# Channel-major copies of the input rows for the first RMSNorm of a hybrid encoder layer, in place of transposes on TensorE

## The chip, the cores and the metric

The kernel runs on one core of a Trainium2 chip. The metric is the device time of one execution in microseconds (us). Three runs of the kernel before took 3526.61, 3523.47 and 3514.22 us; the median is 3523.47 us. The engines are called as the profile calls them: PE is TensorE (PEld its weight loads), DVE VectorE, ACT ScalarE, POOL GpSimd, and SP the engine whose queue issues most of the DMAs.

## The reference

The reference is one layer over two streams, a prompt of 16 learned meta tokens and 2048 new rows, and a sample stream of 64 rows that goes on from given states. Rows have 1024 channels.

```python
def _rmsnorm(x, w):
    y = xf * lax.rsqrt(jnp.mean(jnp.square(xf), -1, keepdims=True) + EPS)
    return (y * w.astype(F32)).astype(x.dtype)
...
m, ns = _mixer(_rmsnorm(x, p['norm1_w'][l]), l, *st, segs, p)
x = x + m
x = x + _swiglu(_rmsnorm(x, p['norm2_w'][l]), p['w_gate'][l], p['w_up'][l], p['w_down'][l])
```

`_mixer` begins with one product of the normed rows with `w_in` (1024 x 5384). Its columns go to three groups of heads (Mamba-2 SSD, RWKV-7, HGRN2), whose outputs are normed, joined, and mapped back by `w_out`. A SwiGLU feed-forward network with 2816 hidden channels and a last RMSNorm follow. The change touches only the first RMSNorm and the way its result reaches the product with `w_in`.

## The kernel before

The 2128 rows are cut into 17 tiles: tile 0 holds the 64 sample rows and the 16 meta rows, tiles 1 to 16 hold 128 prompt rows each. Tiles are gathered into six chunks of 336, 384, 384, 384, 384 and 256 rows, and chunks into three blocks of two.

All large products run in split single precision: each operand is kept as a rounded part `hi` and a remainder `lo`, and PE adds `hi*hi + hi*lo + lo*hi`. A weight unit (128 x 512) is loaded from HBM as `raw` (line 219), rounded by ACT (line 220), and its remainder is taken by POOL for three units of four and by DVE for the fourth (line 222). The split copy is stored to HBM (line 224) and read back when the unit is used again (line 216). There are three `raw` buffers and five for split units.

A chunk goes to the projection as `hT`, a pair of tiles `hhi` and `hlo` with channels on the partitions, 8 groups of 128 channels by up to 384 rows. `Chunk.load` makes it from row tiles with rows on the partitions. For each tile, ACT squares the rows and sums them (line 237); DVE and POOL turn the sum into `(mean + eps)^-0.5` (lines 228 and 230); DVE multiplies the rows by that factor and by the norm's weights, which a DMA has laid down on all partitions (line 246); PE transposes eight blocks of 128 x 128, four to a PSUM bank (line 252); ACT rounds each bank into `hhi` (line 254) and DVE writes the remainder to `hlo` (line 255). A chunk of three tiles has 24 transposes. The pool of PSUM banks `g` has four banks, for the projection's sums and the transposes together.

The row tiles come by DMA on SP's queue (line 144) into three buffers `x`. `Chunk.fetch` asks for the three tiles of a chunk.

`projection` writes the order of the work down: for block 0, the first four column tiles (the "head") of chunk 0, then the load of chunk 1, the head of chunk 1, then the other column tiles with each weight unit used for both chunks. At the end of a block the gate columns `z` are computed, and the load of the next block's first chunk is woven into them. The load of the second chunk of a block comes after the `v` columns of the first. While the projection runs, two streams of mixer work are stepped in between by a table of estimated costs. Below that, a planner that keeps an estimated timeline orders the instructions of each engine and of the DMA queues; priority goes by the order in which the program is written. So an edit in one place can reorder rows on every engine.

SP's queue is in order: where a DMA has to wait until its target buffer is free or its source is written, the DMAs behind it wait as well.

## Time and profile before

| | |
|---|---|
| median of three runs | 3523.47 us |
| time of the profiled execution | 3511.97 us |
| its span in the trace | 3510.2 us |
| mean granted clock of PE | 0.982 |
| busy share: PE, PEld, DVE, ACT, POOL | 96%, 84%, 63%, 35%, 22% |
| DMA over the span | 860.42 MB, 245 GB/s |

The profiled execution is one of the program's faster ones: its own time is 11.5 us under the median, and lies 1.8 us over its span. In the prediction the sum is made against 3511.97 us and then moved up by 11.5 us. A line number in the profile is a line of the kernel; line 111 is the helper through which every product goes, so its groups have to be told apart by the names of their tiles. A name on the left of the arrow is what an instruction writes, the names on the right are what it reads, with the moving operand of a product first.

### The profile page before, as it was taken

How to read it: one execution, taken by the hardware profiler on the slowest of the kernel's cores; microseconds unless marked ns; L12 is line 12 of the kernel's file. 1: busy time of each engine (PE TensorE's matmuls, PEld its weight loads, DVE VectorE, ACT ScalarE, POOL GpSimd, SP SyncE). 2: the span in 40 equal slices, each digit the busy share in tenths (PEclk: the TensorE clock that was granted, in tenths of full speed). 3: DMA queues.
4: the chain of work that ended last, by engine and by line, in shares of the span. 5: the costliest groups of instructions: out<-in, count | busy, mean ns of one | idle time of the engine just before them, and what ended most of it. 6: DMA issues, size and time to landing. Idle time of an engine off the chain costs nothing.

```text
span 3510.2 us, 61013 instructions
## 1 busy us (share of the span) xinstructions
PE 3366.0 (96%) x22588; PEld 2942.8 (84%) x22588; DVE 2212.6 (63%) x4961; ACT 1226.9 (35%) x2635; POOL 778.5 (22%) x1122
## 2 busy tenths in 40 slices
PE   7999999999999998899898999999999999999998
PEld 7999789999799996787787888888988887888786
DVE  3358555567665677687877767667643676665453
ACT  4445233344343443343452212223210352233342
POOL 3324201102112112344442211111100123431101
PEclk9999999999999998899999999999999999999999
DMA  9776875565775667889889898686788567875856
GB/s 321 233 227 209 298 237 160 172 180 163 247 223 173 193 194 245 288 305 315 293 303 346 297 328 275 227 285 203 224 259 267 199 209 263 304 273 165 295 191 215
DMA packets 427123, 860.42 MB, mean 245 GB/s; under 512 B 112432, under 2 KB 212280, under 8 KB 424776
## 3 DMA queue, kind: packets, MB, share of 16 engines
q1 hardware_dynamic: 394376, 749.01, 64.9%
q0 software_dynamic: 32448, 107.50, 8.4%
q8 instruction: 178, 2.92, 0.3%
q14 instruction: 121, 0.99, 0.1%
HBM read 603.81 MB, written 252.54 MB: 244 GB/s over the span
## 4 chain that ended last, share of the span: by engine, by line
PE 69%; DMA 11%; DVE 10%; issue 4%; ACT 2%; POOL 2%; SPq 2%; POOLq 0%; DVEq 0%; ACTq 0%
PE g L111 47%; PE d L111 11%; PE c L111 5%; PE h L111 4%; DMA w<-w 3%; DMA raw<-in_w_up 1%; DMA hin<-hg 1%; POOL w L222 1%; DMA hg<-stage 1%; DVE tp L640 1%; DVE Xp L641 1%; DMA raw<-in_w_gate 1%; PE po L111 1%; DVE acc L1278 1%; DVE gcv L418 1%
## 5 line engine op out<-in xcount | busy, mean ns | idle before, releaser
L111 PE MATMUL g<-hhi,w 128*128 128x384 f32 (+3 forms) x3312 | 831.7, 330 | 10.1 <-POOL w L222 3.7
L111 PEld LDWEIGHTS g<-hhi,w 128*128 128x128 f32 (+1 forms) x3312 | 580.0, 188 | 23.9 <-POOL w L222 4.5
L111 PE MATMUL g<-h2hi,w 128*128 128x384 f32 (+1 forms) x2112 | 548.6, 335 | 21.9 <-DMA w<-w 7.9
L111 PE MATMUL g<-hlo,w 128*128 128x384 f32 (+3 forms) x1680 | 550.5, 328 | 0.0
L111 PEld LDWEIGHTS g<-h2hi,w 128*128 128x128 f32 x2112 | 376.4, 190 | 35.2 <-ACT w L220 8.6
L111 PE MATMUL g<-h2lo,w 128*128 128x384 f32 (+1 forms) x1056 | 349.6, 331 | 0.0
L111 PEld LDWEIGHTS g<-hlo,w 128*128 128x128 f32 (+1 forms) x1680 | 314.1, 187 | 6.2
L222 POOL TENSOR_TENSOR w<-raw,w 128x512 fp32r<-128x512 f32 x180 | 244.0, 1358 | 338.3 <-ACT w L220 276.3
L111 PE MATMUL g<-w,mhi 128*128 128x512 f32 x792 | 259.3, 404 | 8.3 <-DMA w<-w 3.5
L220 ACT ACTIVATE w<-raw 128x512 fp32r<-128x512 f32 x240 | 150.1, 628 | 194.2 <-PE g L111 50.0
L111 PEld LDWEIGHTS g<-h2lo,w 128*128 128x128 f32 x1056 | 200.3, 190 | 2.8
L111 PE MATMUL g<-w,hhi 128*128 128x512 f32 (+1 forms) x544 | 178.1, 407 | 7.4 <-DMA w<-w 4.2
L111 PEld LDWEIGHTS g<-w,mhi 128*128 128x128 f32 x792 | 145.0, 189 | 43.6 <-DVE acc L1278 4.5
L640 DVE TENSOR_TENSOR tp<-Xp,b4k 128x60 f32<-128x60 f32 (+24 forms) x527 | 125.1, 237 | 52.0 <-DMA b4k<-psc 38.9
L1278 DVE TENSOR_TENSOR acc<-g,acc 128x512 f32<-128x512 f32 (+1 forms) x198 | 132.1, 682 | 39.2 <-PE g L111 38.9
L111 PE MATMUL g<-w,mlo 128*128 128x512 f32 x396 | 155.7, 394 | 0.0
L111 PE MATMUL g<-w,op 128*128 128x512 f32 x600 | 142.8, 395 | 0.0
L111 PEld LDWEIGHTS g<-w,op 128*128 128x128 f32 x600 | 112.3, 187 | 27.3
L641 DVE TENSOR_TENSOR Xp<-Xp,tp 128x60 f32<-128x60 f32 (+24 forms) x527 | 122.9, 233 | 13.3
L230 POOL TENSOR_TENSOR rs<-ss,half 128x1 f32<-128x1 f32 (+2 forms) x51 | 34.6, 681 | 424.6 <-DVE ss L228 261.0
L111 PEld LDWEIGHTS g<-w,hhi 128*128 128x128 f32 (+1 forms) x544 | 99.5, 189 | 32.4 <-DMA w<-w 6.5
L356 DVE SCALAR_TENSOR_TENSOR stage<-graw,cvec,stage 128x384 f32<-128x384 f32 (+2 forms) x98 | 53.5, 549 | 113.5 <-ACT graw L351 34.4
(449 smaller groups left out, 6619.2 us busy)
## 6 DMA issues: line engine op xcount, KB each, us to landing
w<-w SPq DMA_DIRECT2D x893, 512.0 KB, 4.4
hin<-hg SPq DMA_DIRECT2D x16, 1280.0 KB, 7.7
rin<-rw SPq DMA_DIRECT2D x16, 896.0 KB, 6.2
raw<-in_w_gate SPq DMA_DIRECT2D x56, 256.0 KB, 4.4
raw<-in_w_up SPq DMA_DIRECT2D x56, 256.0 KB, 4.3
hg<-stage SPq DMA_DIRECT2D x64, 192.0 KB, 2.5
raw<-in_w_out SPq DMA_DIRECT2D x48, 256.0 KB, 4.4
sin<-ss SPq DMA_DIRECT2D x16, 768.0 KB, 4.9
```

Source lines behind the costliest of these rows:

```text
L111: return T.matmul(out, lhsT, rhs, start=start, stop=stop, skip_group_check=more)
L220: S.activation(hi, raw, AF.Copy)
L222: (G if units[0] % 4 < GLO else V).tensor_tensor(lo, raw, wt[:, 0], SUB)
L230: G.tensor_tensor(rs[:n], ss[:n], half[:n, 0:w], ALU.pow)
L356: V.scalar_tensor_tensor(st[:, a0:a1], raw[:, s0:s0 + a1 - a0], mu, st[:, a0:a1], MUL, ADD)
L418: V.scalar_tensor_tensor(cvt[:, :M], raw[:, j:j + M], tap(j), cvt[:, :M], MUL, ADD)
L640: V.tensor_tensor(tv, _bc(Xp[:, 0:m, q], 2, w), _bc(Up[:, q, q + 1:32], 1, m), MUL)
L641: V.tensor_tensor(Xp[:, 0:m, q + 1:32], Xp[:, 0:m, q + 1:32], tv, ADD)
L1278: V.tensor_tensor(self.acc[:n, i, cs], ps[:n], self.acc[:n, i, cs], ADD)
```

## The change

Each chunk's input rows are laid down in HBM a second time by the host, transposed: `xt0` to `xt5`, with channels on the partitions. `Chunk.fetch` now starts two kinds of load. The row tiles go, as before, through SP's queue, but one after the other into a single buffer `xq` (for chunk 0 into three buffers `b4k`); ACT squares each in place and leaves only the sums of squares `xss`. The transposed rows go by two DMAs into one buffer `xT` for a whole chunk.

`Chunk.load` turns all sums of a chunk into factors at once (one POOL power). For each tile, DVE multiplies the identity by the factors (a diagonal 128 x 128 matrix); PE multiplies a matrix of ones by it, which puts the factor of every row on all partitions; ACT copies that out of PSUM as `rb`. For each of the eight channel groups DVE multiplies `xT` by the norm's weight of the channel and by `rb`; for each pair of groups ACT rounds into `hhi` and DVE writes the remainder to `hlo`. The diagonal and `rb` take two of the three `stage` buffers, which also carry projection results to their stores. The buffer that held the norm's weights on all partitions is gone; they are columns of the constants `cvec` now. The matrix of ones is made ahead of the first load.

```diff
-    def fetch(tiles):
...
+    def squares_of(tiles, buf):
+        ss = mk(gp, [P, 4], tag="xss", bufs=2)
...
+        for j, t in enumerate(tiles):
+            xt = buf()
             for src, r0, n in x_rows(t):
                 nc.sync.dma_start(xt[r0:r0 + n], src)
-            xs.append(xt)
-        return xs
+            xt = xt[:LEN[t]]
+            S.activation(xt, xt, AF.Square, accum_out=ss[:LEN[t], j:j + 1])
+        return ss
+    def turned_rows(ci):
+        xT = mk(gp, [P, KD, CW], tag="xT", bufs=1)
+        n = sum(LEN[t] for t in CHUNKS[ci])
+        for k in range(0, KD, 4):
+            nc.sync.dma_start(xT[:, k:k + 4, :n], A[f"xt{ci}"][:, k:k + 4])
+        return xT
...
-    x0 = fetch(CHUNKS[sbs[0][0]][:1])
-    nw1 = norm_rows(gp, "norm1")
+    c0 = sbs[0][0]
+    ss0 = squares_of(CHUNKS[c0], lambda: mk(mx, [P, 1024], tag="b4k", bufs=3))
+    xT0 = turned_rows(c0)
...
         def fetch(self):
-            self.x = fetch(self.tiles)
+            self.ss = squares_of(self.tiles, lambda: mk(gp, [P, D], tag="xq", bufs=1))
+            self.xT = turned_rows(self.ci)
         def load(self):
             hi, lo = self.hT = [mk(gp, [P, KD, CW], F32R, tag=tag, bufs=2) for tag in ("hhi", "hlo")]
-            hs = [(xt[:, :512], xt[:, 512:]) for xt in self.x]
+            N, xT, ss = self.N, self.xT, self.ss
+            nt = self.nt
+            V.tensor_scalar(ss[:, :nt], ss[:, :nt], 1.0 / D, EPS, MUL, ADD)
+            rs = mk(gp, [P, 4], tag="xrs", bufs=2)
+            G.tensor_tensor(rs[:, :nt], ss[:, :nt], half[:, 0:nt], ALU.pow)
+            dg, rb = by(self.stage(), P), self.stage()
             for j, n in enumerate(self.lens):
-                o = self.offs[j]
-                rms_scaled(gp, self.x[j], n, nw1, hs[j], hi[:n, :, o:o + P])
-                yield 0.0
-                for k4 in range(2):
-                    transposed(hs[j][k4], k4, n, hi, lo, o, gbank)
-                    yield 0.5
+                V.tensor_scalar(dg[:n, j, :n], ident[:n, :n], rs[:n, j:j + 1], None, MUL)
+            yield 1.0
+            ps = gbank()
+            for j, n in enumerate(self.lens):
+                mm(ps[:, self.offs[j]:self.offs[j] + n], ones[:n], dg[:n, j, :n], True, True)
+            S.activation(rb[:, :N], ps[:, :N], AF.Copy)
+            yield 1.0
+            for k in range(0, KD, 2):
+                for i in (k, k + 1):
+                    V.scalar_tensor_tensor(xT[:, i, :N], xT[:, i, :N], c("norm1")[:, i:i + 1], rb[:, :N], MUL, MUL)
+                S.activation(hi[:, k:k + 2, :N], xT[:, k:k + 2, :N], AF.Copy)
+                V.tensor_tensor(lo[:, k:k + 2, :N], xT[:, k:k + 2, :N], hi[:, k:k + 2, :N].bitcast(F32), SUB)
+                yield 1.0
```

How the order of the instructions moves is shown at three places. In the changed kernel line 146 is the row load, 156 the load of the transposed rows, 231 the load of a raw weight unit, 236 the store of a split one, 329 the mean, 334 the diagonal, 343 the product with `rb`, 345 the remainder, and 379 the last step of a column tile of the RWKV group.

The first place is SP's queue while the head of chunk 0 is computed. Before, from the second raw unit on:

```order
L219 DMA raw_330<-in_w_rw 128x512
L219 DMA raw_363<-in_w_rw 128x512
L144 DMA x_517<-in_x_prompt 128x1024
L144 DMA x_519<-in_x_prompt 128x1024
L144 DMA x_521<-in_x_prompt 128x1024
L224 DMA w_315<-w_310 128x1024
L219 DMA raw_382<-in_w_rw 128x512
L224 DMA w_367<-w_362 128x1024
L224 DMA w_334<-w_329 128x1024
L219 DMA raw_415<-in_w_rw 128x512
L219 DMA raw_434<-in_w_rw 128x512
```

The same place in the change, in two pieces: from the second raw unit on, and from the eighth raw unit on.

```order
L231 DMA raw_303<-in_w_rw 128x512
L231 DMA raw_336<-in_w_rw 128x512
L146 DMA xq_491<-in_x_prompt 128x1024
L236 DMA w_288<-w_283 128x1024
L231 DMA raw_355<-in_w_rw 128x512
L156 DMA xT_500<-in_xt 128x1536
...
L231 DMA raw_407<-in_w_rw 128x512
L146 DMA xq_494<-in_x_prompt 128x1024
...
L231 DMA raw_459<-in_w_rw 128x512
L146 DMA xq_497<-in_x_prompt 128x1024
```

Before, the three row tiles of chunk 1 left together ahead of the fourth raw unit; now the second follows the sixth raw unit and the third the eighth, with both halves of the transposed rows in between.

The second place is DVE at the load of chunk 1. Before (`x_517`, `x_519` and `x_521` are its three row tiles, `hlo_524` its remainder):

```order
L246 SCALAR_TENSOR_TENSOR x_517<-x_517,rs_57_528,nw_85 128x512 x2
L228 TENSOR_SCALAR ss_546<-ss_546 128x1
L246 SCALAR_TENSOR_TENSOR x_519<-x_519,rs_61_549,nw_85 128x512 x2
L228 TENSOR_SCALAR ss_567<-ss_567 128x1
L246 SCALAR_TENSOR_TENSOR x_521<-x_521,rs_65_570,nw_85 128x512 x2
...
L255 TENSOR_TENSOR hlo_524<-g_532,hhi_523 128x4x128
L255 TENSOR_TENSOR hlo_524<-g_539,hhi_523 128x4x128
```

The same load in the change:

```order
L329 TENSOR_SCALAR xss_490<-xss_490 128x3
L334 TENSOR_SCALAR stage_508<-ident,xrs_506 128x128 x3
L379 SCALAR_TENSOR_TENSOR stage_478<-graw_477,cvec,stage_478 128x64
L379 SCALAR_TENSOR_TENSOR stage_478<-graw_477,cvec,stage_478 128x272
L343 SCALAR_TENSOR_TENSOR xT_500<-xT_500,cvec,stage_509 128x384 x8
L345 TENSOR_TENSOR hlo_504<-xT_500,hhi_503 128x768 x4
```

All eight products with `rb` now stand ahead of the first remainder, and nothing of the chunk starts before the sums of all three tiles are there.

The third place is PE at the load of chunk 5 in the change; `g_10606` receives the factors, `hhi_10597` and `hlo_10598` are the chunk's parts, `g_10675` and `g_10676` its first sums:

```order
L111 MATMUL h_10524<-us_10434,onesr 128x256 x2
L111 MATMUL h_10532<-Sss,sin_10167 128x256 x2
L111 MATMUL g_10606<-stage_10602,onesr 128x128 x2
L111 MATMUL h_10631<-us_10338,us_10247 128x256 x2
L111 MATMUL g_10675<-w_10677,hhi_10597 128x512 x2
L111 MATMUL g_10676<-w_10677,hhi_10597 128x512 x2
L111 MATMUL h_10701<-us_10626,onesr 128x512
L111 MATMUL h_10701<-us_10627,onesr 128x512
L111 MATMUL g_10675<-w_10677,hlo_10598 128x512
```

Where 16 transposes of the chunk stood, 15 of them close together ahead of its first products, there are now two products with ones. The row tiles of chunks 2 to 5 move the other way: their loads and squares stand on SP and ACT within the first part of block 0, since they need no other buffer than `xq`.

More of the change, by code (lines that the diff above doesn't have):

```diff
@@ L136, in x_rows @@
         return [(A["x_prompt"][(t - 1) * P:t * P, :], 0, P)]
-    def fetch(tiles):
-        xs = []
-        for t in tiles:
-            xt = mk(gp, [P, D], tag="x", bufs=3)
+    def squares_of(tiles, buf):
+        ss = mk(gp, [P, 4], tag="xss", bufs=2)
+        if tiles[0] == 0:
+            G.memset(ss, 1.0)
+        for j, t in enumerate(tiles):
+            xt = buf()
             for src, r0, n in x_rows(t):
                 nc.sync.dma_start(xt[r0:r0 + n], src)
-            xs.append(xt)
-        return xs
+            xt = xt[:LEN[t]]
[7 more added lines that the diff above has]
+        return xT
     def norm_rows(p, name, tag="nw"):
@@ L231, in inv_rms, with rms_scaled @@
         return rs
-    def rms_scaled(p, xt, n, wbc, hs, dump=None):
+    def rms_scaled(p, xt, n, wbc, hs):
         ss = mk(p, [P, 1], tag="ss", bufs=2)
-        if dump is not None:
-            S.activation(dump, by(xt[:n], P), AF.Square, accum_out=ss[:n])
-        else:
-            s2 = mk(p, [P, 2], tag="s2", bufs=2)
-            for k4 in range(2):
-                S.activation(hs[k4][:n], xt[:n, k4 * 512:k4 * 512 + 512], AF.Square, accum_out=s2[:n, k4:k4 + 1])
-            V.tensor_tensor(ss[:n], s2[:n, 0:1], s2[:n, 1:2], ADD)
+        s2 = mk(p, [P, 2], tag="s2", bufs=2)
+        for k4 in range(2):
+            S.activation(hs[k4][:n], xt[:n, k4 * 512:k4 * 512 + 512], AF.Square, accum_out=s2[:n, k4:k4 + 1])
+        V.tensor_tensor(ss[:n], s2[:n, 0:1], s2[:n, 1:2], ADD)
         rs = inv_rms(p, ss, n, 1, 1.0 / D, EPS)
@@ L500, in body @@
     first = chunk[sbs[0][0]]
-    first.x = x0 + fetch(first.tiles[1:])
+    first.ss, first.xT = ss0, xT0
     def g1(cis, fn, w, cts, after=None):
@@ L1035, in body @@
     RWA = 64
+    onesr = const("onesr", [P, P], F32R)
+    one_ = mk(mx, [P, P], tag="sg", bufs=1)
+    G.memset(one_, 1.0)
+    V.tensor_copy(onesr, one_)
+    ones = onesr.bitcast(F32)
     flow(first.load())
@@ L1710, in _tm_units, with _turned @@
     return np.ascontiguousarray(w.reshape(kt // ku, ku, P, n).transpose(0, 2, 1, 3).reshape(kt // ku, P, ku * n))
+def _turned(g, ci):
+    x = np.concatenate([g["x_sample"][0], g["meta_tokens"], g["x_prompt"][0]], axis=0)
+    at = np.cumsum([0] + LEN)
+    x = x[at[CHUNKS[ci][0]]:at[CHUNKS[ci][-1] + 1]]
+    return x.T.reshape(KD, P, -1).transpose(1, 0, 2)
 def prep(inp):
@@ L1717, in prep @@
     w = g["w_in"][0]
+    for ci in range(len(CHUNKS)):
+        A[f"xt{ci}"] = _turned(g, ci)
     A["x_prompt"] = g["x_prompt"][0]
```

13 lines of the change are left out of this document (5 added, 8 removed).

## The prediction

> **What bounds the kernel now.** First the page, for the span, the busy shares and the chain that ended last.
>
> ```profile
> span 3510.2 us, 61013 instructions
> PE 3366.0 (96%) x22588; PEld 2942.8 (84%) x22588; DVE 2212.6 (63%) x4961; ACT 1226.9 (35%) x2635; POOL 778.5 (22%) x1122
> PE 69%; DMA 11%; DVE 10%; issue 4%; ACT 2%; POOL 2%; SPq 2%; POOLq 0%; DVEq 0%; ACTq 0%
> ```
>
> PE is busy for 96% of the span and makes 69% of the chain; its idle time is 144 us (3510.2 - 3366.0). What a chunk's load is worth depends on the stage it stands in, so next come the busy times by stretches (columns: stretch, length, then PE, PEld, DVE, ACT, POOL busy with counts, PE's clock, DMA share, GB/s), the first four of 100 us, the last two of 10 us.
>
> ```profile
> 0.00:100.00 100.00, 79.03 (x459) 75.70 (x460) 36.09 (x76) 42.15 (x89) 38.21 (x91) 0.98 0.90 311
> 100.00:200.00 100.00, 100.00 (x630) 95.34 (x630) 43.52 (x105) 43.46 (x93) 30.26 (x56) 1.00 0.73 229
> 400.00:500.00 100.00, 95.06 (x616) 75.49 (x615) 56.38 (x132) 38.06 (x87) 14.31 (x18) 0.97 0.79 269
> 900.00:1000.00 100.00, 95.72 (x728) 80.78 (x728) 67.98 (x174) 39.13 (x97) 17.50 (x22) 0.98 0.75 256
> 50.00:60.00 10.00, 6.88 (x39) 6.37 (x38) 0.62 (x1) 2.11 (x4) 2.89 (x5) 1.00 1.05 406
> 60.00:70.00 10.00, 10.00 (x62) 10.00 (x62) 1.84 (x3) 4.23 (x8) 4.52 (x8) 1.00 1.00 354
> ```
>
> Two regimes are to be seen. In the first 60 us PE starves (21 us of the 144 lie in the first 100) while the DMA engines are full. From 60 us on PE is saturated, and about the later chunk loads it loses some 4 to 5 us in 100. The same view for line 252 alone, the transposes (columns: PE and PEld busy, clock, DMA):
>
> ```profile
> 0.00:100.00 100.00, 8.86 (x48) 7.09 (x48) 0.98 0.90 311
> 400.00:500.00 100.00, 7.15 (x48) 5.44 (x48) 0.97 0.79 269
> 900.00:1000.00 100.00, 6.28 (x40) 4.50 (x40) 0.98 0.75 256
> ```
>
> So the transposes that go are 22.3 us of PE: chunks 0 and 1 in the starved start, chunks 2 and 3 near 450 us, 4 and 5 near 940 us.
>
> **The change part by part.** The prices come from the groups by line and form, and three rows of the timeline (start, length):
>
> ```profile
> L111 PE MATMUL c<-sg,g 128*128 128x128 f32 x136 | 18.6, 281 | 0.0
> L246 DVE SCALAR_TENSOR_TENSOR x<-x,rs,nw 128x512 f32<-128x512 f32 x32 | 24.9, 822 | 3.1 <-POOL rs L230 3.0
> L255 DVE TENSOR_TENSOR hlo<-g,hhi 128x512 fp32r<-128x512 f32 x32 | 21.4, 684 | 4.5 <-ACT hhi L254 4.4
> L254 ACT ACTIVATE hhi<-g 128x512 fp32r<-128x512 f32 x32 | 18.6, 603 | 7.5 <-PE g L252 7.4
> L237 ACT ACTIVATE hhi<-x 128x1024 fp32r<-128x1024 f32 x16 | 16.9, 1056 | 6.0 <-DMA x<-in_x_prompt 4.4 <-POOL w L222 1.2 <-PE g L111 0.2
> L356 DVE SCALAR_TENSOR_TENSOR stage<-graw,cvec,stage 128x384 f32<-128x384 f32 x56 | 35.4, 633 | 64.3 <-ACT graw L351 32.7 <-issue 8.9 <-POOL Xp L621 7.2
> L340 ACT ACTIVATE stage<-g,omu 128x384 f32<-128x384 f32 x56 | 32.4, 579 | 97.7 <-PE g L111 85.7 <-issue 11.3 <-DMA rw<-stage 0.6
> L230 POOL TENSOR_TENSOR rs<-ss,half 128x1 f32<-128x1 f32 x16 | 9.9, 620 | 53.8 <-DVE ss L228 29.7 <-DVE Xp L641 13.0 <-DVE At L816 4.8
> 10.34 0.19 ACT L237 ACTIVATION_READ_ACCUMULATOR hhi<-x 128x1 f32 x1
> 13.01 0.15 DVE L228 TENSOR_SCALAR ss<-ss 128x1 f32<-128x1 f32 x1
> 437.37 0.23 DVE L543 TENSOR_SCALAR sg<-sg 128x128 f32<-128x128 f32 x1 [0.40 <-ACT sg L542]
> ```
>
> *PE work in chunks 2 to 5.* Gone: 88 transposes, 7.15 + 6.28 = 13.4 us. Added: 11 products of ones with a diagonal, 128 columns of full f32. The nearest row is `c<-sg,g`, 17 tiles of four products, each recorded twice: 18.6 / 68 = 0.27 us each, 3.0 us in all. PE is saturated there, so the difference counts: **-10.4 us**. The Trainium skill, page Perfetto Trace Analysis, section Identifying the Most-Contended Engine, says that matmul busy time misleads and that weight-load busy time is the better measure. By it the gone part would be 5.44 + 4.50 = 9.9 us, less about 3 us for the ones' loads, and the sum 3.5 us higher; the PEld columns above (76% and 81% beside 95% and 96%) leave room for that.
>
> *DVE, ACT, POOL.* A chunk of three tiles took DVE 6 x 0.822 + 6 x 0.684 = 9.0 us; now 8 products (the L356 row) 5.1, four remainders of 768 columns (1.5 x 0.684 = 1.03) 4.1 and three diagonals 0.7: 9.9 us. ACT goes from 6.8 us to 7.4 (three squares 3.2, `rb` 0.58, four roundings at 1.5 x 0.603). POOL does one power of 0.62 in place of three. DVE and ACT are busy 40 to 70% in these stretches, so the work as such is **0**, hidden under PE's products; uncovered it would be 1.5 us a chunk. What counts is the order: eight products ahead of the first remainder.
>
> *Waits at the loads of chunks 2 to 5.* PE's waits in the stretch 200 to 500 us (first two rows) and 900 to 1000 us (last three), us in total, times, longest:
>
> ```profile
> PE g L111 <- DVE hlo L255: 1.2, 1, 1.2
> PE g L252 <- ACT stage L391: 0.5, 1, 0.5
> PE g L111 <- DVE hlo L255: 1.9, 1, 1.9
> PE g L252 <- DVE hlo L255: 1.0, 1, 1.0
> PE g L252 <- ACT stage L391: 0.8, 1, 0.8
> ```
>
> These 5.4 us go. For chunks 2 and 4 the new chain is woven into the gate columns, which cover it. For chunks 3 and 5 PE has the ones close ahead of the chunk's own products, and only `hi` products and some mixer work until the first `lo` is there. For chunk 3 that is 0.58 + 5.1 + 1.03 = 6.7 us plus some 2 us of mixer work on DVE in between, for chunk 5 (256 rows, two thirds) 4.5 plus 2. I count PE's cover from the order as about 5.5 us (six products of `hi`, 16 mixer transposes) and 2 us: 3 + 4.5 = 7.5 us of new waits. Together **+2 us**; the bounds are -5.4 (all covered) and +9.8 (nothing covered, 15.2 - 5.4).
>
> *The start.* These rows of the timeline and of the DMAs of the first 70 us carry it (the DMA rows end in KB each and us to landing):
>
> ```profile
> 19.43 0.58 PE L111 MATMUL g<-hhi,w 128*128 128x336 f32 x2 [0.78 <-POOL w L222]
> 33.55 0.50 SPq L219 DMA_DIRECT2D raw<-in_w_rw  x1
> 43.69 0.41 PE L111 MATMUL g<-hhi,w 128*128 128x384 f32 x1 [1.17 <-DVE stage L356]
> 50.70 0.44 PE L111 MATMUL g<-hhi,w 128*128 128x384 f32 x1 [0.50 <-DMA w<-w]
> 55.69 0.44 PE L111 MATMUL g<-hhi,w 128*128 128x384 f32 x1 [2.62 <-DMA w<-w]
> DMA packets 12196, 23.38 MB, mean 334 GB/s; under 512 B 2320, under 2 KB 5776, under 8 KB 12190
> w<-w SPq DMA_DIRECT2D x21, 512.0 KB, 7.5
> x<-in_x_prompt SPq DMA_DIRECT2D x8, 512.0 KB, 5.9
> ```
>
> Ahead of the first raw unit the change puts `xT0` (128 x 8 x 336 x 4 B = 1.38 MB) in place of the norm row laid on all partitions (0.52 MB): 0.86 MB, at 334 GB/s 2.6 us. PE's steady start moves from 19.43 to about 22. The head of chunk 0 then goes at the pace of the weights, without the 24 transposes of chunk 1 (24 of the 48 in the first 8.86 us), and ends near 42 as before. The load of chunk 1 decides. Its third row tile is issued right behind the eighth raw unit (33.55 before), say at 34, since it waits for the square of the second in the same buffer; SP's later weight reads stand behind it. Landing after 5.9: 40. Then in a row: square with its sum read 1.25, mean 0.15, power 0.62, diagonals 0.7, ones 0.8, `rb` 0.58, eight products 5.1, first remainder 1.03, and about 1 us between engines: 51. Before, steady products began at 43.69, with waits of 0.5 and 2.62 us for weights read back, which by 51 have landed. 7.3 - 3.1 gives **+4 us**. It is 0 if the weights set the pace in both kernels. It is 12 if every added byte up to 60 us (`xT0`, 1.57 MB each for chunks 1 and 2, less 0.52, 4.0 MB) delays a weight.
>
> *Early row tiles of chunks 3 to 5.* Eight loads of 0.52 MB move into the first part of block 0, with squares on ACT and a wait on SP between any two. PE is full there with DMA at 0.73 of its time after 100 us, and up to five split units lie ahead: **0**; uncovered, see the second rival.
>
> Sum on the profiled execution's own 3511.97 us: -10.4 + 2 + 4 = -4.4, so 3507.6. That execution lies 11.5 us under the median of 3523.47, which gives **3519 us** for a median of runs.
>
> **The rivals.** *The start is free* and the loads' waits vanish: -10.4 - 5.4 = -15.8, 3507.7 us. For it: the first 60 us wait for POOL's and DMA's weights, and three powers per chunk no longer stand on POOL's queue between weight units. Against it: the third tile's chain is serial and its order is written out above.
>
> *Transfers become the bound until the first block has its weights.* In the first part of block 0, by the order up to some 150 us, the change moves 8.2 MB more (the 4.0 above and eight row tiles), 24.6 us at 334 GB/s, all through SP's one queue, where a row tile that waits for ACT's square holds weights behind it. It decides if the free DMA share after 60 us (about a quarter) cannot be used, because SP stands still for longer than the five split units last. -10.4 + 2 + 24.6 = +16.2: 3540 us, slower. For it: DMA share 1.05 and 1.00 around 60 us. Against it: PE waits for nothing from 100 to 200 us at 0.73.
>
> *The transposes cost less than their busy time*, because they overlapped their neighbours. Priced by their weight loads, 9.9 us go and 3 come: -6.9 + 2 + 4 = -0.9, 3522.6 us, no change. It is what the Trainium skill's rule above comes to. For it speaks that 0.16 us of busy time per transpose (22.3 / 136) stands beside 0.13 us of weight load (17.0 / 136); against it that a wait for an operand or a bank comes on top of both.
>
> **How the numbers follow.** Chances: the forecast 0.46, the free start 0.27, the transfers 0.14, cheap transposes 0.13. A measurement of this kernel tells 0.3%, some 10.6 us, from no change: under 3512.9 is faster, over 3534.0 slower. Faster: 0.25 of the free start and 0.08 of the forecast's lower end, 0.33. Slower: 0.12 of the transfers and 0.06 of the upper ends of the start's and the waits' bounds, 0.18. No change: 0.49. The order of mixer and feed-forward work also shifts by rows on all engines between 400 and 2700 us, with no sign that I can read; it widens the range by some us on either side. The range 3503 to 3536 takes in the free start and the upper bound of the start (3519 + 8 + that spread), and leaves out most of the transfers' case.
>
> **What would show it.** Right: line 252 left with the 72 transposes of the other norm; PE 5 to 10 us less busy in 400 to 500 and 900 to 1000 together; the first 384-row product later than 43.69, steady only near 51; new waits of products for `hlo` at chunks 3 and 5. Wrong: PE steady before 47 us (free start), or PE waiting for `w` or `raw` between 70 and 200 us (transfers), or the ones' products far from 0.27 us.

## The result, and the profile after

The change makes the kernel slower. Its median is 3557.59 us (six runs, 3549.23 to 3562.40) beside 3523.69 us for the kernel before on the same chip (3514.22 to 3526.61); the ratio is 1.0097 with an interval of 1.0079 to 1.0115. The forecast was 3519 us with a range of 3503 to 3536, so the time lies 39 us above the one and 22 above the other's upper end.

First the page of the changed kernel: span, busy times, and the shares of the chain that ended last.

```profile
span 3560.2 us, 60750 instructions
PE 3375.6 (95%) x22486; PEld 2946.3 (83%) x22486; DVE 2208.7 (62%) x4971; ACT 1238.3 (35%) x2633; POOL 777.7 (22%) x1112
PE 54%; DMA 17%; DVE 13%; issue 8%; POOL 3%; ACT 2%; SPq 2%; POOLq 0%; DVEq 0%; ACTq 0%
```

PE has 102 records fewer, as the change says, and yet it is busy for 9.6 us longer (3375.6 against 3366.0), with 184.6 us idle against 144.2. PE's share of the chain fell from 69% to 54%. Work was taken away, and yet PE both waits longer and is busy longer.

How that can be is seen in the stretches that the prediction showed of before (same columns: stretch, length, PE, PEld, DVE, ACT, POOL busy with counts, PE's clock, DMA share, GB/s).

```profile
0.00:100.00 100.00, 69.14 (x361) 66.17 (x362) 34.79 (x76) 45.36 (x89) 36.28 (x81) 0.93 0.96 336
100.00:200.00 100.00, 100.00 (x630) 95.43 (x629) 42.54 (x95) 46.04 (x100) 33.19 (x63) 1.00 0.81 263
400.00:500.00 100.00, 93.43 (x655) 72.72 (x655) 62.49 (x145) 38.45 (x84) 16.59 (x18) 0.97 0.78 267
900.00:1000.00 100.00, 93.84 (x698) 74.63 (x697) 66.98 (x197) 33.22 (x82) 12.95 (x15) 0.95 0.74 243
```

In the first 100 us PE lost 10 us of busy time and its clock stands at 0.93 in place of 0.98; in the stretch about chunk 5 the clock is 0.95 in place of 0.98. So time is lost in two ways: PE waits, and after a wait it works at a lower clock. I therefore took, for every stretch of 2 us, PE's busy time times its clock as **work at the full clock**, the rest of its busy time as **loss at the low clock**, and what is left as **idle**, and summed them between instructions that both kernels have (names with the lines of the kernel before): the 25th copy of an RWKV column (line 340, 133 us), the last copy of a gate column `z` (line 395, 1367 us), and the last product of the feed-forward network's gate with its `up` column (line 1242, 2713 us). Both kernels were profiled a second time (the runs `b_again` and `a_again` below); the table has the means of the two profiles, in us.

| stretch | before | after | difference | idle | low clock | work |
|---|---|---|---|---|---|---|
| start to 133 | 134.5 | 144.0 | +9.6 | +9.8 | +3.7 | -3.9 |
| projection and mixer, 133 to 1367 | 1238.9 | 1237.1 | -1.8 | +4.9 | +3.0 | -9.6 |
| mixer, output and feed-forward, 1367 to 2713 | 1350.0 | 1377.2 | +27.2 | +18.9 | +5.6 | +2.6 |
| 2713 to the end | 798.2 | 799.5 | +1.3 | +1.1 | +0.9 | -0.6 |
| sum | 3521.6 | 3557.7 | +36.1 | +34.7 | +13.1 | -11.6 |

The sum, +36.1, is near the difference of the medians (+34). The saved work is there, 11.6 us. Against it stand 35 us of idle time and 13 us lost to the clock, and three quarters of the whole lie in a stretch that the change does not touch.

**The start.** Rows of the timeline of the changed kernel (start, length, and in brackets the idle time before it and what ended it):

```profile
16.90 1.38 SPq L231 DMA_DIRECT2D raw<-in_w_rw  x3
22.36 0.65 PE L111 MATMUL g<-hhi,w 128*128 128x336 f32 x1 [7.39 <-ACT w L232]
40.98 0.33 SPq L146 DMA_DIRECT2D xq<-in_x_prompt  x1
52.40 0.41 PE L111 MATMUL g<-hhi,w 128*128 128x384 f32 x1 [2.95 <-DMA w<-w]
55.37 0.69 PE L111 MATMUL g<-hlo,w 128*128 128x384 f32 x1 [2.56 <-DVE hlo L345]
```

and what SP waited for in its first 20 us:

```profile
SPq L106 <- DMA xT<-in_xt: 1.8, 1, 1.8
SPq L1074 <- DMA xT<-in_xt: 1.8, 1, 1.8
SPq L106 <- DMA b4k<-in_x_prompt: 0.8, 1, 0.8
```

The first weights leave SP at 16.90 (before: 13.45). In its first 20 us SP stands still three times until a large load has landed, 4.4 us in all; the kernel before has three such waits as well, of 0.9, 0.8 and 0.7 us, so that 2.0 of the 3.5 us lie there. The first product of chunk 0 runs at 22.36 (before: 18.08). The third row tile of chunk 1 leaves at 40.98, where I had put it at 34, and the products of chunk 1 run steadily from 55.4, where I had put 51.

**The load of chunk 3.** Rows of the timeline, and PE's busy time and clock by 2 us, of the same place of the changed kernel:

```profile
480.35 0.94 PE L111 MATMUL g<-stage,onesr 128*128 128x128 f32 x6
480.94 1.28 DVE L626 TENSOR_TENSOR L<-c,rwmask 128x512 f32<-128x512 f32 x2
482.81 4.31 DVE L343 SCALAR_TENSOR_TENSOR xT<-xT,cvec,stage 128x384 f32<-128x384 f32 x8
483.70 2.44 ACT L930 ACTIVATE dec<-dec,cu 128x128 f32<-128x128 f32 x8 [1.83 <-DMA dec<-cu]
486.05 1.56 ACT L344 ACTIVATE hhi<-xT 128x768 fp32r<-128x768 f32 x2
486.93 2.93 PE L111 MATMUL g<-w,hhi 128*128 128x512 f32 x6 [3.12 <-ACT hhi L344]
490.66 3.55 DVE L345 TENSOR_TENSOR hlo<-xT,hhi 128x768 fp32r<-128x768 f32 x4
```

```profile
482.00:484.00 2.00, 1.69 (x32) 1.30 (x30) 2.00 (x6) 0.30 (x1) 0.00 (x0) 1.00 0.30 92
484.00:486.00 2.00, 0.00 (x0) 0.00 (x0) 2.00 (x5) 2.00 (x8) 0.00 (x0) 1.00 0.00 0
486.00:488.00 2.00, 1.07 (x3) 0.89 (x4) 2.00 (x5) 2.00 (x4) 0.00 (x0) 0.70 0.01 4
488.00:490.00 2.00, 2.00 (x7) 1.37 (x6) 2.00 (x4) 2.00 (x3) 0.16 (x1) 0.50 0.33 49
490.00:492.00 2.00, 2.00 (x17) 1.84 (x16) 2.00 (x4) 1.46 (x4) 1.11 (x2) 0.95 0.19 45
```

From the end of the three products of ones (480.35 + 0.94) to the end of the first remainder (490.66 + 0.89) pass 10.3 us, where I had worked out 8.7: eight steps of the mixer's decay (`dec`) stand on ACT ahead of the first rounding, and mixer work on DVE between the products and the remainders. PE waits 3.12 us for the first `hhi`, and its clock stands at half for 3.41 us, from 486.80 to 490.21.

**Mixer and feed-forward.** PE's waits in that stretch (total, times, longest): the longest group for weights read back, and the five longest that concern the bank `h`. Of the kernel before:

```profile
PE g L111 <- DMA w<-w: 19.2, 16, 3.6
PE h L111 <- ACT us L920: 4.4, 2, 2.3
PE h L973 <- DVE At L822: 3.7, 2, 2.8
PE h L843 <- DVE At L839: 2.1, 1, 2.1
PE h L111 <- DVE tp L640: 2.0, 1, 2.0
PE h L111 <- DVE hin L832: 1.8, 4, 0.8
```

Of the changed kernel:

```profile
PE g L111 <- DMA w<-w: 23.4, 15, 2.9
PE h L111 <- ACT us L943: 7.6, 4, 3.2
PE h L111 <- DVE us L962: 4.6, 3, 3.6
PE h L111 <- DVE dec L998: 4.1, 2, 3.5
PE h L111 <- DVE hin L855: 3.6, 4, 1.5
PE h L111 <- DVE Xp L664: 3.4, 1, 3.4
```

`h` is the bank of the HGRN2 and Mamba-2 stream. All waits of its products sum to 18.8 us before and 37.0 after (18.6 and 30.4 in the second profiles); those for the weights read back grew by 4.2 (2.4 in the second profiles). No single wait is long: PE's queue has the products of that stream at places where their operands are not ready yet.

### The profile page after: what moved, and what is told of

Same layout as the page of the kernel before. It is cut to its first block, busy times and chain, and to the rows that moved or that the text cites. A ratio compares the mean times of both kernels' runs of the same rounds, so it can differ in the third digit from the quotient of the medians.

```text
span 3560.2 us, 60750 instructions
## 1 busy us (share of the span) xinstructions
PE 3375.6 (95%) x22486; PEld 2946.3 (83%) x22486; DVE 2208.7 (62%) x4971; ACT 1238.3 (35%) x2633; POOL 777.7 (22%) x1112
## 4 chain that ended last, share of the span: by engine, by line
PE 54%; DMA 17%; DVE 13%; issue 8%; POOL 3%; ACT 2%; SPq 2%; POOLq 0%; DVEq 0%; ACTq 0%
PE g L111 38%; PE d L111 7%; PE c L111 4%; DMA w<-w 3%; PE h L111 3%; DMA raw<-in_w_down 2%; DMA hin<-hg 2%; DMA raw<-in_w_up 1%; DMA raw<-in_w_gate 1%; DVE tp L663 1%; DMA hg<-stage 1%; DVE Xp L664 1%; POOL w L234 1%; DVE gcv L441 1%; DMA dec<-cu 1%
## 5 line engine op out<-in xcount | busy, mean ns | idle before, releaser
L111 PE MATMUL g<-h2hi,w 128*128 128x384 f32 (+1 forms) x2112 | 550.4, 336 | 21.8 <-DMA w<-w 11.9
L111 PE MATMUL g<-w,op 128*128 128x512 f32 x600 | 142.8, 396 | 0.0
L111 PE MATMUL d<-ya,w 128*128 128x512 f32 x528 | 124.5, 392 | 1.2 <-DMA w<-w 1.2
```

The lines of the kernel that those rows point to most:

```text
L111: return T.matmul(out, lhsT, rhs, start=start, stop=stop, skip_group_check=more)
```

## The experiments

Theories at the outset: **A**, the start costs 10 us, by a serial chain through one buffer `xq`; **B**, the bookkeeping: a load now yields six units of cost and not three, which moves the two mixer streams against the projection, and costs the 27 us; **C**, these 27 us are the luck of the order: any edit draws a new order of mixer and feed-forward work, and the orders differ by 10 us and more. Later came **D** (the loads of chunks 3 and 5), **E** (the RWKV stream, which runs 60 to 80 us late in the changed kernel, costs the 27 us), **F** and **G** (what delays the weights at the start). The last table of this section has the stretches of every run. Each ratio is to the kernel before, timed beside the run on the same chip; its median there was 3521.59 to 3528.62 us, so differences in us between two runs are good to some 5 us, and the ratios compare better.

### Is one profile enough?

Both kernels, unchanged, once more.

> The kernel before, unchanged, profiled a second time, to see how far two executions of one program differ stage by stage. The first profile lies 12 us under the median of its runs. If executions differ everywhere by a little: about 3524 us, the start (the first 133 us of the first profile) within 4 us of it, and PE's idle time, its loss at the low clock and its work at the full clock (144.2, 47.6 and 3318.5 us) within 8, 5 and 2 us. If the feed-forward stretches 1400 to 2700 us, which move by up to 30 us between kernels, also move by 10 us and more between executions of one program, what the first profiles show there says little.

> The change, unchanged, profiled a second time. Its first profile: PE idle 184.6 us, 67.6 us lost to the low clock, work at the full clock 3308.0. If the causes are in the program: 40 us more idle and 20 us more low-clock loss than the kernel before, within 8 us, and PE 10 us late at 130 us. If the first profile was a bad one: 10 to 20 us less in the feed-forward stretches, about 3545 us.

The kernel before took 3534.74 us in this run and the change 3556.98. The kernel before had 157.6 us idle, 54.7 at the low clock, 3320.6 of work; the change 186.5, 60.8 and 3307.9. Two executions of one program differ by 5 to 9 us between 1367 and 2713 us and by some 2 us at the start. Between 133 and 1367 us they differ by 8 and 10 us. So the 27 us are no accident of one execution, and a difference below some 10 us in one profile says nothing. The idle time of the kernel before moved by 13 us and not by the 8 that I had allowed.

### The bookkeeping

`a_half` is the change, `b_double` the kernel before, with one number changed in `Chunk.load` (in `a_half` at its three places):

```diff
-            yield 1.0
+            yield 0.5
```

```diff
-                    yield 0.5
+                    yield 1.0
```

> The change, with one edit: the three `yield 1.0` in Chunk.load become 0.5. A chunk's load then counts 3 in the table of estimated costs, as before, and no longer 6, so that the two streams of mixer work stand against the projection as they did before; no work is added or taken away. Theory B (the bookkeeping: the HGRN2 stream was pulled ahead and the RWKV stream fell behind, which costs the feed-forward stage some 20 to 27 us): about 3533 us, 25 under the change's 3557.6, and the feed-forward stretches 1400 to 2700 us fill up again. Theory A (the start and the loads of the later chunks cost it): within 5 us of 3557.6. Theory C (any new order of the mixer and feed-forward work moves the time by 10 us and more with no cause in the change itself): anything from 3530 to 3570, with the loss in other stretches than the change's.

> The kernel before, with one edit: `yield 0.5` in Chunk.load becomes 1.0, so that a chunk's load counts 6 in the table of estimated costs, as in the change; no work is added or taken away. Theory B (bookkeeping): about 3545 us, 20 and more over the kernel before, lost between 1400 and 2700 us. Theory A (start and loads): 3524, the same as before within 5 us. Theory C (any new order moves the time): 3505 to 3550, and no sign that agrees with that of the other run with half the count.

`a_half` took 3562.03 us (ratio to before 1.0098, 1.0074 to 1.0121), the same as the change; `b_double` 3514.68 (0.9968, 0.9951 to 0.9984), faster than before and not slower. **B falls, with the wrong sign.** The bookkeeping does move the time, though: `b_double` has no other work and the same order up to 400 us.

Does that gain hold, and does it go with the count? `b_double2` is the same kernel again; `b_triple` counts three times over.

> The kernel before with each load counted double, a second time and with more rounds: the run above gave a ratio of 0.9968 (0.9951 to 0.9984). Theory C (the order alone is worth some tenths of a per cent): 0.995 to 0.999 again, since the order of the instructions is the same. If that was chance of the executions: 0.999 to 1.001.

> The kernel before with each load counted three times over (`yield 1.5` for 0.5), a third neutral edit of the kernel before. Theory C: another draw of the order, idle time and low-clock loss between 1367 and 2713 us anywhere from 110 to 145, total 3510 to 3550; no trend with the factor is expected (once 3526, twice 3515, chunk 5 alone twice 3527). If the count itself mattered: below 3515.

`b_double2`: 0.9981 (0.9969 to 0.9993), smaller, but there. `b_triple`: 1.0001 (0.9985 to 1.0017), so no trend with the count.

The same edit for the load of chunk 5 alone leaves the order as it was up to 900 us:

```diff
-            yield 1.0
+            yield 0.5 if self.ci == 5 else 1.0
```

> The change, with one edit: in the load of chunk 5 alone the three `yield 1.0` become 0.5. No work is added or taken away, and the order of the instructions is that of the change up to about 900 us; from there on the two streams of mixer work fall in other places between the projection and the feed-forward network. Theory C (the 26 us that the change loses between 1360 and 2705 us are the luck of the order, which any edit draws anew): the idle time of PE and its loss at the low clock between 1367 and 2713 us, 139 and 144 us in two profiles of the change and 113 and 121 in two of the kernel before, come out anywhere from 110 to 145; the total from 3530 to 3565. Theory E (the RWKV stream, late by 60 to 80 us in the change, costs it there): 135 or more again, total 3550 to 3565.

> The kernel before, with the load of chunk 5 alone counted double (`yield 1.0` for 0.5); the order is that of the kernel before up to about 900 us. Theory C: idle time and low-clock loss between 1367 and 2713 us anywhere from 110 to 145, total 3510 to 3550. Theory E: within 113 to 121 as before, total within 8 us of the kernel before.

`a_l5`: 3547.27 us (1.0064, 1.0047 to 1.0080), 10 less than the change, with 132 us of idle time and low clock between 1367 and 2713. `b_l5`: 3527.33 (1.0001, 0.9983 to 1.0019), with 131 us where the kernel before has 113 and 121. E wanted 135 or more for the one and at most 121 for the other; 132 is too near to tell, 131 is against it. C's range, 110 to 145, was so wide that it could hardly miss. In `a_l5` the RWKV stream is 46 us late at 1953 us in place of 84, and the loss fell; but in the runs `b4k1` and `early` below it is 71 and 77 us late and the loss is as small as before. **E does not hold.** C is left, and what speaks for it are the runs in which the work stays and the time moves.

### One half of the change at a time

`old01` loads chunks 0 and 1 as before and the others as in the change; `new01` the other way round.

```diff
+OLD = {0, 1}
...
         def fetch(self):
+            if self.ci in OLD:
+                self.x = fetch_rows(self.tiles)
+                return
```

> The change for chunks 2 to 5 alone; chunks 0 and 1 are loaded as before (rows on the partitions, transposes). The three row tiles of a chunk lie in the buffer of `xT`, the norm's row in that of `xq`, since both ways do not fit beside each other otherwise. Theory A (the start costs some 10 us, a serial chain through one buffer `xq`): PE's lag of 10 us at 100 to 200 us is gone, and the time is about 3547; if the -10.4 us of PE work of chunks 2 to 5 were also to be seen, 3537. Theory B (bookkeeping of the later loads): still 3545 to 3550, with the loss between 1400 and 2700 us. Theory C: the lag is gone at 400 us and comes back, of any size and sign, later.

> The change for chunks 0 and 1 alone; chunks 2 to 5 are loaded as before. Theory A: the lag of 10 us at 100 to 200 us stays to the end, so about 3534 us, and nothing more is lost at the loads of chunks 3 and 5. Theory B (bookkeeping of the later loads): the same 3534, since only the loads of chunks 0 and 1 count more. Theory C: 10 us behind at 400 us, and of any sign after that, 3515 to 3555.

`old01`: 3532.15 us (1.0014, 0.9999 to 1.0030). `new01`: 3546.10 (1.0055, 1.0034 to 1.0076). The start's loss goes with chunks 0 and 1: up to the copy at 133 us `new01` takes 142.8 us and `old01` 138.0, which is within what six profiles of kernels without the change show (133.3 to 138.1). Between 133 and 1367 `old01` takes 1230.2 us, in the middle of the kernels without the change (1224.7 to 1243.7), though its work there is 11 us less (1181.8 against 1192.7): idle time and low clock eat it up. That holds for every run: in this stretch the profiles of kernels with the new loads of chunks 2 to 5 have 1178 to 1184 us of work and 48 to 58 of idle time and low clock, those without 1188 to 1197 and 31 to 51. Beyond its start `new01` loses in its one profile 5 us between 133 and 1367 and 9 after that, and it changed nothing there.

### The loads of chunks 3 and 5

`early` makes the factors and the products with `rb` while the `v` columns of the chunk before are computed, and puts the diagonals and `rb` into the buffer `xq`.

```diff
-            dg, rb = by(self.stage(), P), self.stage()
+            q = mk(gp, [P, D], tag="xq", bufs=1)
+            dg, rb = by(q[:, 0:CW], P), q[:, 512:512 + CW]
...
-            yield from head(sb[0])
+            yield from weave(head(sb[0]), *[chunk[ci].prep() for ci in sb[1:] if si])
```

> The change, with two edits: the diagonals and `rb` lie in the buffer `xq` and no longer in two of the three `stage` buffers; and for chunks 3 and 5 the factors, the product of ones and the eight products with the norm's weights are made ahead, woven into the `v` columns of the chunk before, so that the load is left with four roundings and four remainders. Theory D (the load of the second chunk of a block is a serial chain on DVE, ACT and `stage`, for which PE waits some 4 us and then works at half the clock for as long again, 9 us at chunk 3 and 9 at chunk 5): the lag steps up by no more than 2 us at chunks 3 and 5, PE's clock stays at 1.00 there, and the time is about 3540 us, 16 to 18 under the change. Theory A alone (start): within 5 us of 3557.6. Theory C (the new order of mixer and feed-forward work): the steps at the loads are gone, but the total is anything from 3525 to 3565.

3538.72 us (1.0032, 1.0014 to 1.0050), 19 under the change, which is D's number. But the stretches do not say what D says. From 960 to 1000 us, where chunk 5 is loaded, PE's longest waits (total, times, longest) are in the change the first three of these rows. `early` has only the last two:

```profile
PE h L111 <- DVE Sss L978: 2.6, 1, 2.6
PE g L111 <- DVE stage L334: 1.3, 1, 1.3
PE h L111 <- DVE dec L968: 0.9, 1, 0.9
PE c L111 <- DVE b4k L734: 0.5, 1, 0.5
PE h L111 <- ACT us L954: 0.4, 1, 0.4
```

The lag behind the first profile of before (copies of `v` columns, line 391, on both sides of a load) no longer jumps at chunk 5 (13.0 us ahead of it, 10.3 after it; in the change 11.6 and 21.8), where the clock now stays at 1.00. At chunk 3 the step is smaller, 3 us (8.7 and 11.8; in the change 4.3 and 12.9), but the clock still falls to half there, against D:

```profile
486.00:488.00 2.00, 2.00 (x8) 1.49 (x6) 2.00 (x4) 1.37 (x4) 0.00 (x0) 0.50 0.22 79
```

And from 133 to 1367 us the kernel takes 1234.8 us, the change 1241.2 and 1233.0, with 52 us of idle time and low clock in place of 58 and 50: the smaller steps do not show in the stretch. The 19 us come after 1367: 1355.9 us in place of 1374.6 and 1379.7. **D is right on the step at chunk 5, in part at chunk 3, and wrong on its worth.**

Whether the gain goes with the edit or with the order is asked by `old01_early`, the same edit on `old01`.

> The change for chunks 2 to 5 alone, as in the run with chunks 0 and 1 loaded as before, and in addition the early factors and products for chunks 3 and 5, with diagonals and `rb` in `xq`. If start and loads are what a design can mend: no lag at 130 us, no steps at chunks 3 and 5, PE's work at the full clock 5 to 8 us under the kernel before; about 3515 us, 10 under the kernel before, if the feed-forward part falls out as there (idle time and low-clock loss of 113 to 121 us); 3515 to 3540 by the luck of the order.

3548.59 us (1.0065, 1.0042 to 1.0089). The edit that took 19 us from the change adds 16 to `old01`, 8 of them after 1367 us in its one profile (1369.7 against 1361.5). One edit with opposite signs on two kernels fits C, and not a fixed worth of the edit.

### What makes the start

`b4k1` puts the row tiles of chunk 1 into three buffers:

```diff
-            self.ss = squares_of(self.tiles, lambda: mk(gp, [P, D], tag="xq", bufs=1))
+            self.ss = squares_of(self.tiles, lambda: mk(mx, [P, 1024], tag="b4k", bufs=3) if self.ci == 1 else mk(gp, [P, D], tag="xq", bufs=1))
```

> The change, with one edit: the row tiles of chunk 1 go to the three buffers `b4k`, as those of chunk 0, and no longer one after the other through the one buffer `xq`. No other chunk changes. Theory A (the serial chain through one buffer sets PE's steady start): the third row tile leaves before 30 us in place of 41, products of chunk 1 start before 47 us in place of 52.4, and the lag of 10 us at 130 us falls to 5: about 3552 us. If the late first weights of chunk 0 set it (raw units leave SP 3.5 us late, first product 4.3 us late, and PE then at half the clock): the lag stays at 8 to 10 us and the time at 3557.

Rows of its timeline:

```profile
28.34 0.17 DVE L329 TENSOR_SCALAR xss<-xss 128x3 f32<-128x3 f32 x1 [4.77 <-ACT b4k L148]
45.49 1.70 DVE L334 TENSOR_SCALAR stage<-ident,xrs 128x128 f32<-128x128 f32 x3
54.80 0.44 PE L111 MATMUL g<-hhi,w 128*128 128x384 f32 x1 [3.31 <-ACT hhi L344]
```

The sums of all three tiles are there at 28.34 (in the change at 47.03), but on DVE the diagonals stand behind the last steps of the third column tile of chunk 0's head, which begin at 44.15, and are made at 45.49; PE starts the chunk at 54.80. **The serial chain through `xq` is not what holds it.** The time, 3542.42 us (1.0046, 1.0026 to 1.0066), is 15 under the change with a start that is 2 us longer: in the profile the gain lies after 1367 us (1354.4), one more draw.

`xt1late` holds back the transposed rows of chunk 1, `xt0act` issues those of chunk 0 on ACT's queue:

```diff
         xT = mk(gp, [P, KD, CW], tag="xT", bufs=1)
+        if ci == 1:
+            G.tensor_copy(xT[:, 0, 0:1], carry[:, 1:2])
+            G.tensor_copy(xT[:, 4, 0:1], carry[:, 1:2])
```

```diff
-            nc.sync.dma_start(xT[:, k:k + 4, :n], A[f"xt{ci}"][:, k:k + 4])
+            (nc.sync if ci else nc.scalar).dma_start(xT[:, k:k + 4, :n], A[f"xt{ci}"][:, k:k + 4])
```

> The change, with the transposed rows of chunk 1 (1.57 MB) held back: POOL writes one element of each half of `xT` from `carry`, which the second column tile of chunk 0 writes, and so the two DMAs stand behind the eighth raw weight unit in SP's queue and no longer behind the fourth. Theory F (the head of chunk 0 goes at the pace of the weights, and each byte that moves ahead of a weight delays it): raw units five to eight leave SP 2 to 5 us earlier, the last column tile of the head is copied out near 44 us in place of 48.7, and the lag at 130 us falls from 10.5 to some 6. Theory A (the serial chain of the load of chunk 1): the lag stays at 10 or grows, since `xT` comes later. The total goes by the luck of the order as well, 3535 to 3560.

> The change, with the two DMAs of `xT0` (1.38 MB) issued on ACT's queue and no longer on SP's. The same bytes move. Theory G (SP stands still between 8 and 13 us because the large loads ahead of the constants have not landed, and so the first weights leave 3.5 us late; PE then waits 7.4 us and falls to the low clock): the first raw units leave SP near 14 us in place of 16.8, the first product runs near 19 in place of 22.1, and the lag at 130 us falls from 10.5 to 6 or 7. Theory F (bytes): the raw units leave earlier but land no earlier, and the lag stays at 10. Total 3525 to 3560 by the luck of the order.

Of `xt1late` (3532.36 us; 1.0016, 1.0002 to 1.0029) two rows:

```profile
48.80 0.94 PE L111 MATMUL g<-stage,onesr 128*128 128x128 f32 x6 [1.95 <-DVE stage L337]
55.30 0.66 PE L111 MATMUL g<-hhi,w 128*128 128x384 f32 x1 [5.56 <-DMA w<-w]
```

The eighth raw unit leaves 2.6 us earlier (37.06 against 39.69), and then PE waits 5.56 us for a weight that is read back, until 55.30. The start stays at 144.8 us. The whole time, with the same work and the same start, is 25 us under that of the change. Of `xt0act` (3551.11; 1.0081, 1.0066 to 1.0096) again two, then the largest group of SP's waits in the first 20 us (total, times, longest), and half a microsecond from it (columns as above):

```profile
18.39 1.28 SPq L231 DMA_DIRECT2D raw<-in_w_rw  x3
22.59 0.65 PE L111 MATMUL g<-hhi,w 128*128 128x336 f32 x1 [6.00 <-ACT w L232]
SPq L106 <- DMA xT<-in_xt: 7.1, 2, 4.0
12.50:13.00 0.50, 0.00 (x0) 0.00 (x0) 0.05 (x1) 0.50 (x2) 0.02 (x1) 1.00 0.02 5
```

On another queue the same bytes go first, and the first weights leave at 18.39, later still. The edit was to spare SP its waits, but SP waits for the same two loads for 7.1 us in place of 3.6, and from 12.5 to 13.5 us the DMA engines move 4 to 5 GB/s, next to nothing. So this run does not test G: whether SP's standing still costs something beyond the bytes stays open.

`old0` loads chunk 0 alone as before (`OLD = {0}`), `old1` chunk 1 alone.

> Chunk 0 loaded as before, chunks 1 to 5 as in the change. Theory G (the late first weights of chunk 0 make the start's cost): raw units leave SP near 14 us, and the lag at 130 us is 2 to 5. If the load of chunk 1 makes it by itself (its chain of squares, diagonals, ones, products and remainders, and the weights read back behind its rows): the head of chunk 0 ends as before, near 43 us, the steady products of chunk 1 start near 52 to 55 all the same, and the lag at 130 us is 8 to 10.

> Chunk 1 loaded as before, chunks 0 and 2 to 5 as in the change. Theory G: raw units leave SP near 16.8 us, the first product runs near 22, and the lag at 130 us is 8 to 10, as the head goes at the pace of its weights. If the load of chunk 1 makes the cost: the first product is late by 4 us, but the lag at 130 us is no more than 4 to 6.

They took 3534.13 and 3549.46 us, one execution each. The start is 141.6 us long with the new load of chunk 1 alone, 146.3 with that of chunk 0 alone, and 144 with both. The two costs do not add: against 134.5 they are 7 and 12 us, and 10 together. Neither expectation has these numbers (2 to 5 or 8 to 10 for the first, 8 to 10 or at most 6 for the second). Three things end together near 55 us: the head of chunk 0, the chain of chunk 1's load, and the weights read back. In each of these runs another of them held PE when one was moved, and of all that was tried only `old01` and `old01_half` below (138.0 and 137.5), with both loads as before, took most of the cost away; `old01_early`, with the same loads of chunks 0 and 1, still has 141.7.

### Is there a version that wins?

`old01_half` is `old01` with `a_half`'s number.

> The change for chunks 2 to 5 alone, as in the run with chunks 0 and 1 as before (3532 us), with the three `yield 1.0` of the load halved, so that every load counts 3. No work is added or taken away. Theory C (luck of the order): idle time and low-clock loss between 1367 and 2713 us anywhere from 110 to 145 (125 in that run), total 3510 to 3550. Up to 1367 us within 4 us of that run. It is also the likeliest of these to beat both kernels, if the order falls well.

3527.00 us (1.0008, 0.9995 to 1.0021): no difference from the kernel before. No version with the change beat it. The one kernel that did, `b_double`, has nothing of the change.

The stretches of all runs, in us (idle and low clock: in the stretch from 1367 to 2713; two profiles where there are two; `old0` and `old1` have no ratio, being one execution each). A profile is one execution: that of `xt1late` took 10 us more than its median.

| kernel | ratio to before | start | 133 to 1367 | 1367 to 2713 | idle and low clock |
|---|---|---|---|---|---|
| before | 1 | 133.3, 135.6 | 1234.1, 1243.7 | 1345.5, 1354.4 | 113, 121 |
| `b_double` | 0.9968, 0.9981 | 137.2, 137.2 | 1231.2, 1234.3 | 1347.0, 1354.2 | 110, 118 |
| `b_triple` | 1.0001 | 135.8 | 1224.7 | 1364.3 | 132 |
| `b_l5` | 1.0001 | 138.1 | 1236.0 | 1357.7 | 131 |
| after | 1.0097 | 143.9, 144.1 | 1241.2, 1233.0 | 1374.6, 1379.7 | 139, 144 |
| `a_half` | 1.0098 | 144.6 | 1229.9 | 1382.1 | 145 |
| `a_l5` | 1.0064 | 144.1 | 1237.4 | 1361.5 | 132 |
| `b4k1` | 1.0046 | 146.1 | 1236.0 | 1354.4 | 119 |
| `xt1late` | 1.0016 | 144.8 | 1230.6 | 1361.6 | 127 |
| `xt0act` | 1.0081 | 148.4 | 1233.2 | 1372.5 | 137 |
| `early` | 1.0032 | 144.0 | 1234.8 | 1355.9 | 115 |
| `old0` | | 141.6 | 1237.3 | 1356.0 | 120 |
| `old1` | | 146.3 | 1239.4 | 1364.2 | 133 |
| `new01` | 1.0055 | 142.8 | 1243.9 | 1359.1 | 127 |
| `old01` | 1.0014 | 138.0 | 1230.2 | 1361.5 | 125 |
| `old01_half` | 1.0008 | 137.5 | 1229.6 | 1359.0 | 116 |
| `old01_early` | 1.0065 | 141.7 | 1232.3 | 1369.7 | 129 |

## Why the prediction was wrong

Against its own baseline the forecast was -4.4 us, and the table above has +36.1. Of the 40 us between them, about 6 are the start, 7 the stretch of the later loads, 27 the stretch of mixer and feed-forward work, for which the sum had no term, and 1 the end.

*PE work of chunks 2 to 5, -10.4 us:* right. Work at the full clock fell by 9.6 us between 133 and 1367 us. A product of ones cost 0.31 us (0.94 for three of them, the row of 480.35) where I had 0.27. The rival that transposes cost less than their busy time would have had 6.9 us, which is further off. The Trainium skill, page Perfetto Trace Analysis, section Identifying the Most-Contended Engine, gives weight-load time as a measure of how near PE is to its peak. Taking it for the price of a few instructions was my own step. The check itself is made of PE's busy time, as the price was. In elapsed time the saving does not show apart from the waits that came with it.

*DVE, ACT, POOL, 0, and early row tiles, 0:* right as far as the rows tell. PE is busy for 100.00 of the 100 us from 100 to 200 with DMA at 0.81, so the rival by transfers, which needed PE to wait there, falls.

*Waits at the loads, +2 us:* mis-sized, inside its bounds of -5.4 to +9.8. Idle time grew by 4.9 us and the loss at the low clock by 3.0, 7.9 together (the two profiles of before differ by 10 us in this sum; but all thirteen profiles with the new loads of chunks 2 to 5 have 48 us or more of it, and of the seven without them only one), so that of -8.4 (-10.4 + 2) only -1.8 was left. Three things were wrong. ACT and DVE had mixer work ahead of the roundings and remainders, which made 8.7 us of chain into 10.3. The wait stood at another place: I had named products waiting for `hlo` at chunks 3 and 5, and there are none; at chunk 3 PE waits 3.12 us for the first `hhi`, at chunk 5 for the diagonals (1.3) and for mixer operands (2.6 and 0.9). And I priced a wait at its length alone.

*The start, +4 us:* mis-sized, at +9.6 and inside its bounds of 0 to 12. The steps that I listed are in the trace, but the first weights were 3.5 us late and not 2.6, the third row tile left at 41 and not at 34, and steady products began at 55.4 and not at 51. That the single buffer `xq` decides, as I argued, is refuted by `b4k1`. Of the 9.6 us, 3.7 are again the low clock. The rival of a free start falls.

*The order of mixer and feed-forward work, "with no sign that I can read; it widens the range by some us":* this is the step that failed. A term put at nothing was +27.2 us, three quarters of the result. Edits that change no work gave 110 to 132 us of idle time and low clock in that stretch to the kernel before, and 132 to 145 to the changed one; `early` and `b4k1`, edits of loads that end before 1000 us, 115 and 119. The same edit (`early`) took 19 us from one kernel and gave 16 to another. So among orders of the changed kernel's work the stretch spans 30 us (115 to 145, single profiles, which differ by 5 to 9 us for one program), and the medians of the seven kernels with all of the change span the same: 1.0016 to 1.0098, 29 us, with starts of 144 to 148. The change as it was written drew near the bad end of these, and that part is luck. It is not all luck: the middle one of the seven, `a_l5`, has 1.0064, some 3546 us, which is over 3536 too, since the start and the waits were sized too low. A range that holds the result would have had to reach 22 us further up. Orders of the kernel before would not have shown that much, as its three neutral edits moved the time by -11 us to nothing.

What stays open is whether the change shifts these draws as a whole. Without it the four kernels have a mean of 124 us (117 for before and 114 for `b_double` with two profiles each, 132, 131); the ten with the new loads of chunks 2 to 5 and no edit of how these are made 130 (two profiles of after counted as one). With a spread of about 10 us among kernels, the 6 us between the means are not told from none. That the products into `h` wait longer is no mark of the change either: 19 us before and 26 to 47 in the kernels with the change, but 35 and 31 in `b_double`, the fastest of all, and 33 in `b_triple`. Nor was it tried apart whether the other places of the buffers in the changed kernel matter there.

## What to carry to other kernels

Where a planner orders the work, an edit that moves any estimate draws a new order of everything behind it. Its worth has to be measured against the spread of orders of the same work, by a few edits that change a number and no work, before a gain or a loss of that size is put down to the edit; here changes of one number moved the kernel before by up to 11 us and the changed one by up to 12, and edits of the loads that leave the work as it is 29, where the change itself was worth 34.

A saving on a full engine is worth its work only while the engine stays fed: some 10 us of PE's work went, and the chain through three engines in place of the transposes left PE waiting, and then slow, for about as long.

## What was not expected of the hardware

A wait of PE costs more than its length. In the rows of the load of chunk 3 above, PE is idle for about 3 us (0.31 us of 482 to 484, all of 484 to 486, 0.93 of 486 to 488), and its clock is half from 486.80 to 490.21. The kernel before shows the same at 446 us, with PE not idle all the time:

```profile
446.00:448.00 2.00, 0.56 (x5) 0.42 (x4) 2.00 (x5) 1.87 (x5) 0.00 (x0) 1.00 0.96 283
448.00:450.00 2.00, 0.81 (x5) 0.53 (x4) 2.00 (x4) 0.69 (x1) 0.00 (x0) 1.00 0.83 310
450.00:452.00 2.00, 2.00 (x7) 1.57 (x6) 2.00 (x5) 2.00 (x5) 0.00 (x0) 0.56 0.07 29
452.00:454.00 2.00, 2.00 (x7) 1.58 (x6) 2.00 (x7) 1.98 (x6) 1.12 (x2) 0.58 0.19 66
454.00:456.00 2.00, 2.00 (x10) 1.62 (x10) 1.92 (x2) 0.73 (x1) 1.88 (x3) 1.00 0.53 197
```

Over the whole program the loss at the low clock is 48 and 55 us before, beside 144 and 158 us of idle time: about a third on top. The Trainium skill, page TensorE: Matmul & The Clock Gate, section What's actually happening, says that the array drops to half its clock after an idle window of some 3.4 us and rises again after as long a busy one. The trace agrees on the half (0.50) and on the length of the slow time (3.41 us in both places); it differs on "idle", since PE was busy for a third of the 4 us from 446 to 450 and the clock fell all the same. In the 20 profiles of this case the clock stands at 1.00 or 0.50 for 3.41 us or multiples of it. Cut into such stretches, each of the 312 at 1.00 in which PE was busy for under 44% was followed by one at 0.50; of the 19,308 in which it was busy for half or more, 103 were. So a stretch in which PE is only half idle can bring on the same slow 3.41 us as a whole wait.
